# A hybrid decoder step: three GLA projection passes that load x already split in two, with sums moved from GpSimd to VectorE and another product order in the attention pass

## The chip, the core and the metric

The kernel runs on one core of a Trainium2 chip. The metric is the device time of one execution in microseconds (us); the times shown are medians of runs. PE is TensorE's matrix multiply, PEld its weight load, DVE is VectorE, ACT is ScalarE, POOL is GpSimd, and SP is the engine whose queue issues nearly all DMAs here.

## The reference

One decoder layer for 2048 prompt tokens and 64 sample tokens (8 sequences of 8), model width 1024, all in float32:

```python
z = jnp.einsum('btd,dn->btn', x, w_in)
q, k, v, g_att, gq, gk, gv, g_gla, g_lr, r_att, r_gla = jnp.split(z, SPLIT_POINTS, axis=-1)
o_att = swa_prompt(q, k, v, attn_sink, rel_table)      # or swa_sample; 8 heads of 64, window 128
log_a = log_sigmoid(g_lr @ w_gk_up + b_gk) / 16
o_gla, S = gla(gq * HK**-0.5, gk, gv, log_a, s0)       # 4 heads, state 128 x 256
o_gla = o_gla * rsqrt(mean(o_gla**2) + EPS) * gla_norm_w
h_att = (o_att * silu(g_att)) @ w_pa
h_gla = (o_gla * silu(g_gla)) @ w_pg
merged = sigmoid(r_att) * h_att + sigmoid(r_gla) * h_gla
x = layer_norm(DN_ALPHA * x + merged @ w_o, ln_g, ln_b)
```

The GLA recurrence of a head, by chunks, with b the running sum of log_a: `o = (q e^b) S + tril((q e^b)(k e^-b)^T) v`, and S is decayed and gains `(k e^(b_last-b))^T v`. Outputs are the new x, the last keys and values, and the states.

## The kernel before

**Products.** Every float32 product is made of three fast ones. An operand a is split into a high part (`xh`, `wh`: a ScalarE cast, line 144) and a low part (`xl`, `wl`: the difference, line 145, on VectorE or GpSimd), and high x high, low x high and high x low are summed in PSUM (lines 1126 to 1128).

**Passes.** The projections go in eight passes: AT (attention columns of `w_in`, five column groups p), G0, G1, G2 (the GLA columns, four groups each), then `w_pa` (half the depth), `w_ra`, `w_rg`, `w_pg`. A pass does a two-by-two block product in seven products instead of eight. Product i uses one combination of x's blocks and one of the weights'; products 1, 2 and 3 use plain blocks of x, the others combinations kept in DRAM (`xc_d`), made once while AT starts. Tokens come in MS = 3 stripes s, so a pass has 7 x 3 units (i, s), and a unit has one group of 12 matmuls per p, 128 x 128 by 128 x 352 (6 in `w_pa`).

**Operands of a unit.** `raw_x` loads 704 KB into a buffer `xs`, `prep_x` splits it into `xh` and `xl`. All three come from one set of seven buffers, `xb`. x's low part is made on VectorE in AT and after G2, on GpSimd in G0, G1 and G2 (`eng=nc.gpsimd`). All seven combinations are the same in AT, G0, G1, G2, w_ra and w_rg. Loads of x are issued up to three units ahead, splits one unit ahead. Weights: `raw_w` loads one to three blocks, `prep_w` combines them on GpSimd (lines 176 to 182) and splits them, a product ahead.

**Combination of the products.** `combine` takes each group out of PSUM. With the order 1, 2, 7, 6, 5, 3, 4, product 1 is copied to `a12`; 2 completes a quadrant; 7 is copied by ScalarE to `a21` (line 239); 6 is added to `a12` (line 242), and GpSimd adds that sum to `a21` (line 243); 5 completes a quadrant (246) and is added to `a12` (247); 3 (250) and 4 (253) complete the last two. A finished quadrant goes to its sink: a store, or a tanh and a VectorE product (`silu_sink`, line 270) and a store.

**Other work on TensorE.** Its order is written out: after each full group of products `tick` issues what stands due at that tick. The attention runs from two ticks before the end of AT to somewhere in G1. The recurrence follows (`chain`), from then to 12 ticks before `w_pg`: one head after another, tile after tile of 128 tokens, in steps of `st` ticks. For a tile, `gla_a` makes the masked matrix A, `gla_v` transposes v and k and has ScalarE copy them (line 891, tiles `ak` and `gv`), `gla_b` multiplies (lines 921 to 924) and starts the norm (`gla_norm`: ScalarE square, line 908, two GpSimd steps on one column, lines 909 and 910, ScalarE scaling into `ring`, line 911), and `gla_c` transposes the normed rows (line 937). `combo` makes the combinations of later passes' operands. Only TensorE's order is fixed by hand; that of the other engines and of SP's queue is laid out when the program is built, from estimated times.

The end, from about 1731 us, is the product with `w_o` and the layer norm.

Of the kernel before, what the change touches and what calls it, by code (L numbers as in the profile page):

```python
# [12 lines left out]
F32 = mybir.dt.float32  # L13
# [8 lines left out]
P = 128  # L22
# [25 lines left out]
GCH = [(i * GT, GT) for i in range(NP // GT - 1)] + [(NP - 2 * P, P), (NP - P, P + NS)]  # L48
GU = GT
NW4 = 10  # L50
ORDER = (1, 2, 7, 6, 5, 3, 4)
FINAL = {2: (0, 0), 5: (1, 1), 3: (0, 1), 4: (1, 0)}


# [1 line left out]
def kernel(ctx, tc, io):  # L56
# [69 lines left out]
    def at(t, fn):  # L126
        side.setdefault(max(int(t), now[0]), []).append(fn)
# [15 lines left out]
    def split(dst_h, dst_l, src, eng=nc.vector):  # L143
        pin["a"] = nc.scalar.copy(dst_h, src)  # L144
        i = eng.tensor_tensor(dst_l, src, dst_h.bitcast(F32), ALU.subtract)  # L145
        if eng is nc.vector:
            pin["d"] = i
# [3 lines left out]

    class Pass:

        def __init__(self, w, kh, np_, src, kept, sinks, parts=None, eng=nc.vector):
            self.w, self.kh, self.np, self.src, self.kept = w, kh, np_, src, kept
            self.sinks, self.parts, self.eng = sinks, parts, eng
            self.A, self.acc = {}, {}

        def wtile(self, tag, p, dt=F32):
# [11 lines left out]
            return out  # L171

        def prep_w(self, i, p, r):
            A, tt = self.A, nc.gpsimd.tensor_tensor
            if i == 7:
                tt(r[0], r[0], r[1], ALU.subtract)  # L176
            elif i == 6:
                tt(r[0], r[0], r[1], ALU.add)  # L178
                tt(r[2], r[0], r[2], ALU.subtract)
                A[p, "s1"], A[p, "s2"] = r[0], r[2]  # L180
            elif i == 3:
                tt(r[0], r[0], A.pop((p, "s2")), ALU.subtract)  # L182
            a = A[p, "s2"] if i == 6 else A.pop((p, "s1")) if i == 5 else r[0]
            hi, lo = (self.wtile(n, p, F32R) for n in ("wh", "wl"))
            split(hi, lo, a)
            return hi, lo

        def raw_x(self, i, s):
            n = self.kh * T
            x = mtile("xb", F32, "xs")[:, :n]  # L190
            if i in (1, 2, 3):
                k, t = {1: (0, 0), 2: (1, 0), 3: (1, 1)}[i]
                if self.src is None:
                    for h in (2 * k, 2 * k + 1):
                        need(ug_d[h], [0], toks(s, t).start, toks(s, t).stop)
                    d = [ug_d[h][:, :, toks(s, t)] for h in (2 * k, 2 * k + 1)]
                else:
                    d = [self.src[:, k * self.kh:(k + 1) * self.kh, toks(s, t)]]
            else:
                assert (id(self.kept), s) in made  # L200
                d = [self.kept[{6: 0, 5: 1, 4: 2, 7: 3}[i]][:, s, :self.kh]]
            m = self.kh // len(d)
            for j, d_ in enumerate(d):
                pin["x"] = nc.sync.dma_start(x.rearrange("p (k t) -> p k t", t=T)[:, j * m:(j + 1) * m], d_)
            return x

        def prep_x(self, i, s, x):
            hl = [mtile("xb", F32R, n)[:, :self.kh * T] for n in ("xh", "xl")]
            split(*hl, x, self.eng)
            return hl  # L210

        def partners(self, i, p, s):
# [9 lines left out]
            nc.sync.dma_start(y.rearrange("p (a t) -> p a t", a=2), d)  # L222
            return [y[:, :T], y[:, T:]]

        def atile(self, p, tag):
            return mtile(tag) if p < 4 else mt("a5", T, 6)

        def combine(self, i, p, s, ps, parts):
            acc, z = self.acc, None
            add = nc.vector.tensor_tensor  # L230
            if i == 1:
                a = acc[p, s, 12] = self.atile(p, "a12")
                nc.scalar.copy(a, ps)
            elif i == 2:
                z = mtile("fin")
                add(z, acc[p, s, 12], ps, ALU.add)
            elif i == 7:
                u = acc[p, s, 21] = self.atile(p, "a21")
                nc.scalar.copy(u, ps)
            elif i == 6:  # L240
                a, u = acc[p, s, 12], acc[p, s, 21]
                add(a, a, ps, ALU.add)  # L242
                pin["p"] = nc.gpsimd.tensor_tensor(u, u, a, ALU.add)  # L243
            elif i == 5:
                a, z = acc[p, s, 12], mtile("fin")
                add(z, acc[p, s, 21], ps, ALU.add)
                add(a, a, ps, ALU.add)
            elif i == 3:
                z = acc.pop((p, s, 12))
                add(z, z, ps, ALU.add)  # L250
            else:
                z = acc.pop((p, s, 21))
                add(z, z, ps, ALU.subtract)
            if z is not None:
                c, t = FINAL[i]
                self.sinks[p](z, parts, p, c, toks(s, t))

    def keep_sink(dst):
# [36 lines left out]
    for h in range(GH):  # L295
        gsinks += [keep_sink(z_kq[h]), keep_sink(z_vv[h]), silu_sink(z_gg[h], nw_h)]
    xT = io["xT"]
    passes = [Pass(io["w_at"], 4, 5, xT, xc_d, [keep_sink(z_kv)] + [keep_sink(z) for z in z_q] +
                   [silu_sink(z) for z in z_ga])]
    passes += [Pass(io[f"w_g{j}"], 4, 4, xT, xc_d, gsinks[4 * j:4 * j + 4], eng=nc.gpsimd) for j in range(3)]  # L300
    passes += [Pass(io["w_pa"], 2, 4, ua_d, ac_d, [store_sink] * 4),
               Pass(io["w_ra"], 4, 4, xT, xc_d, [gated_sink] * 4, parts=ha_d),
               Pass(io["w_rg"], 4, 4, xT, xc_d, [gate_sink] * 4),
               Pass(io["w_pg"], 4, 4, None, uc_d, [merge_sink] * 4, parts=tt_d)]
    P_AT, P_G0, P_G1, P_G2, P_PA, P_RA, P_RG, P_PG = range(8)
    units = [(passes[0], i, s) for s in range(MS) for i in ORDER[:2]]
# [83 lines left out]
    def combo(key, eng):  # L390
        combine_do(*combine_load(combos[key].popleft()), eng)
# [601 lines left out]
    def chain(h, t0, st):  # L993

        at(t0 - 14, lambda: gla_w(h))
        for c, (c0, T_) in enumerate(GCH):
            last = c == len(GCH) - 1
            Tp = T_ - (NS if last else 0)
            nt = Tp // P
            B = dict(h=h, t0=c0, T=T_, Tp=Tp, nt=nt, last=last)  # L1000
            b = t0 + st * (c0 // P)
            at(b - 14, lambda B=B: gla_load(B))
            at(b - 10, lambda B=B: gla_z(B))
            at(b - 10, lambda B=B: gla_load_v(B))
            at(b - 4, lambda B=B: gla_kq(B))
            for i in range(nt):
                o = b + st * i
                at(o, lambda B=B, i=i: gla_a(B, i))
                at(o + st / 4, lambda B=B, i=i: gla_v(B, i))
                at(o + 3 * st / 4, lambda B=B, i=i: gla_b(B, i))  # L1010
                at(o + 3 * st / 2, lambda B=B, i=i: gla_c(B, i, P, i * P))
            at(b + 3, lambda B=B: gla_load_g(B))
            o = b + st * nt
            if last:
                at(o - 5, lambda B=B: samp_state(B))
                at(o - st / 2, lambda B=B: gla_v(B, B["nt"]))
                at(o, lambda B=B: samp_a(B))
                at(o + 1, lambda B=B: nc.sync.dma_start(io["o_sp"][B["h"]], R["S"][sstate[B["h"]]]))
                at(o + 3, lambda B=B: samp_b(B, 0))
                at(o + 5, lambda B=B: samp_b(B, 2))  # L1020
                at(o + 9, lambda B=B: gla_c(B, "s", NS, B["Tp"]))
                at(o + 9, lambda B=B: gla_store(B))
            else:
                at(b + st * (nt + 1 / 2) + 1, lambda B=B: gla_store(B))

    tg = max(tick_of(P_G1) + 2, t_att + 3)
    at(tg, lambda: mpool("cg"))
    at(tg, rings)
# [337 lines left out]
```

## Time and profile before

| | |
|---|---|
| median of 3 runs | 1926.25 us (1920.5 to 1927.8) |
| profiled execution | 1930.8 us, its span 1929.0 us |
| TensorE busy | 1803.9 us, 94% of the span |
| VectorE, ScalarE, GpSimd busy | 69%, 48%, 36% |
| mean granted TensorE clock | 0.978 |
| DMA | 422.65 MB, mean 219 GB/s |

Times are busy times of one profiled execution. A busy TensorE is not TensorE at its peak, since matmuls overlap. In a group's row stand the line, engine, operation, output and inputs, shapes, count, busy us, the mean ns of one, and after the second bar the idle time of the engine before it, with what ended most of it. In a row of a stretch stand its length, each engine's busy us with the count, the granted clock (1.00 is full), the share of time in which the 16 DMA engines worked, and GB/s. A row of waits has who waited, for whom, total us, how many times, and the longest. A helper's line number serves all its callers, so groups are told by their tiles.

### The profile page before, as it was taken

The page shows a single profiled execution, that of the slowest core. Times are in us where ns is not written, and L with a number is a line of the kernel's source. Part 1 is how long each engine was busy: PE and PEld are TensorE (multiplying, and loading weights), DVE is VectorE, ACT ScalarE, POOL GpSimd, SP SyncE. Part 2 cuts the span into 40 slices and gives each one's busy share as a digit, 9 for nine tenths or more (in the row PEclk, how much of TensorE's full clock was granted, in tenths as well). Part 3 has the DMA queues.
Part 4 walks back from the last instruction along what each step waited for, and adds up shares of the span by engine and source line. Part 5 has one row for each costly group of instructions (what it writes and reads, how often), then busy time and mean ns, then how long its engine had stood idle before and what let it go on. Part 6 is the DMA issues. An engine that isn't in the chain of part 4 may idle for free.

```text
span 1929.0 us, 30434 instructions
## 1 busy us (share of the span) xinstructions
PE 1803.9 (94%) x10619; PEld 1638.7 (85%) x10619; DVE 1334.9 (69%) x2372; ACT 921.6 (48%) x1882; POOL 693.3 (36%) x572
## 2 busy tenths in 40 slices
PE   7899989999999998989999999998989999999998
PEld 6699988888878987888888989997889999997886
DVE  5756637787676875658767876887668666876656
ACT  3332235555655455666665656665647433211100
POOL 1253144434344445554424053224342125541111
PEclk9999999999999999999999999999999999999999
DMA  8866766366566676536666987687876888796531
GB/s 301 288 214 207 242 209 200 124 201 209 158 208 205 220 251 208 188 118 183 209 206 180 289 298 229 209 286 267 276 254 204 268 277 281 237 307 222 164 115 55
DMA packets 279641, 422.65 MB, mean 219 GB/s; under 512 B 26509, under 2 KB 221445, under 8 KB 279472
## 3 DMA queue, kind: packets, MB, share of 16 engines
q1 hardware_dynamic: 278560, 419.86, 67.1%
q8 instruction: 84, 1.38, 0.3%
q0 software_dynamic: 832, 0.72, 0.2%
q14 instruction: 69, 0.57, 0.1%
q10 hardware_dynamic: 96, 0.13, 0.0%
HBM read 299.13 MB, written 122.36 MB: 219 GB/s over the span
## 4 chain that ended last, share of the span: by engine, by line
PE 56%; DVE 11%; DMA 10%; ACT 7%; POOL 5%; issue 4%; SPq 1%; DVEq 0%; POOLq 0%; ACTq 0%
PE pd L1126 12%; PE pd L1127 12%; PE pd L1128 11%; PE pd L1173 3%; PE pd L1172 3%; PE pd L1171 3%; DMA ws<-w_g 2%; POOL xl L145 1%; PE pa L587 1%; DVE wl L145 1%; PE pa L621 1%; PE pa L637 1%; DMA x<-ug_d 1%; PE pa L923 1%; DVE xl L145 1%
## 5 line engine op out<-in xcount | busy, mean ns | idle before, releaser
L1126 PE MATMUL pd<-xh,wh 128*128 128x352 f32 x2484 | 854.6, 344 | 35.6 <-ACT xh L144 13.1
L1127 PE MATMUL pd<-xl,wh 128*128 128x352 f32 x2484 | 811.3, 327 | 15.9 <-POOL xl L145 11.6
L1128 PE MATMUL pd<-xh,wl 128*128 128x352 f32 x2484 | 809.9, 326 | 0.1
L1126 PEld LDWEIGHTS pd<-xh,wh 128*128 128x128 f32 x2484 | 476.4, 192 | 85.9 <-issue 32.5
L1127 PEld LDWEIGHTS pd<-xl,wh 128*128 128x128 f32 x2484 | 479.1, 193 | 21.7 <-POOL xl L145 13.2
L1128 PEld LDWEIGHTS pd<-xh,wl 128*128 128x128 f32 x2484 | 475.4, 191 | 0.4 <-DVE wl L145 0.4
L145 POOL TENSOR_TENSOR xl<-xs,xh 128x1408 fp32r<-128x1408 f32 x63 | 206.7, 3281 | 190.5 <-ACT xh L144 164.7
L144 ACT CAST xh<-xs 128x1408 fp32r<-128x1408 f32 (+1 forms) x162 | 208.8, 1290 | 115.7 <-PE pd L1127 101.7
L145 DVE TENSOR_TENSOR wl<-ws,wh 128x512 fp32r<-128x512 f32 (+1 forms) x231 | 200.0, 876 | 62.8 <-ACT wh L144 62.7
L145 DVE TENSOR_TENSOR xl<-xs,xh 128x1408 fp32r<-128x1408 f32 (+1 forms) x99 | 157.8, 1594 | 51.5 <-ACT xh L144 50.6
L144 ACT CAST wh<-ws 128x512 fp32r<-128x512 f32 (+1 forms) x231 | 133.9, 592 | 107.5 <-PE pd L1127 73.5
L243 POOL TENSOR_TENSOR a<-a,a 128x352 f32<-128x352 f32 x99 | 108.5, 1106 | 117.4 <-DVE a L242 104.2
L911 ACT ACTIVATE ring<-pa,sq 128x256 f32<-128x256 f32 (+1 forms) x68 | 32.3, 474 | 168.7 <-POOL sq L910 168.7
L1171 PE MATMUL pd<-woh,x 128*128 128x512 f32 x256 | 101.2, 395 | 0.9 <-ACT woh L144 0.9
L1172 PE MATMUL pd<-woh,x 128*128 128x512 f32 x256 | 101.5, 396 | 0.5 <-DVE x L145 0.5
L1173 PE MATMUL pd<-wol,x 128*128 128x512 f32 x256 | 101.2, 395 | 0.6 <-DVE wol L145 0.6
L178 POOL TENSOR_TENSOR ws<-ws 128x512 f32<-128x512 f32 (+1 forms) x32 | 43.9, 1373 | 152.0 <-DMA ws<-w_pg 36.7
L909 POOL TENSOR_SCALAR sq<-sq 128x1 f32<-128x1 f32 (+1 forms) x68 | 28.6, 421 | 185.2 <-ACT ring L908 185.2
L176 POOL TENSOR_TENSOR ws<-ws 128x512 f32<-128x512 f32 (+1 forms) x32 | 42.3, 1323 | 140.0 <-DVE xl L145 39.5
L601 ACT ACTIVATE s<-s,nm 128x256 f32<-128x256 f32 (+1 forms) x128 | 62.5, 490 | 57.0 <-DVE nm L598 57.0
L144 ACT CAST x<-xst 128x384 fp32r<-128x384 f32 (+2 forms) x48 | 22.3, 486 | 139.3 <-PE pd L1172 104.5
L182 POOL TENSOR_TENSOR ws<-ws 128x512 f32<-128x512 f32 (+1 forms) x32 | 49.6, 1559 | 86.3 <-DMA ws<-w_pa 17.5
(250 smaller groups left out, 2858.1 us busy)
## 6 DMA issues: line engine op xcount, KB each, us to landing
xs<-xc_d SPq DMA_DIRECT2D x72, 704.0 KB
xs<-xT SPq DMA_DIRECT2D x48, 704.0 KB
ws<-w_g SPq DMA_DIRECT2D x108, 256.0 KB
xc<-tt_d SPq DMA_DIRECT2D x48, 352.0 KB
ws<-w_at SPq DMA_DIRECT2D x45, 256.0 KB
ws<-w_ra SPq DMA_DIRECT2D x36, 256.0 KB
ws<-w_rg SPq DMA_DIRECT2D x36, 256.0 KB
ws<-w_pg SPq DMA_DIRECT2D x36, 256.0 KB
```

Of the source, the lines that this page charges most:

```text
L144: pin["a"] = nc.scalar.copy(dst_h, src)
L145: i = eng.tensor_tensor(dst_l, src, dst_h.bitcast(F32), ALU.subtract)
L178: tt(r[0], r[0], r[1], ALU.add)
L182: tt(r[0], r[0], A.pop((p, "s2")), ALU.subtract)
L243: pin["p"] = nc.gpsimd.tensor_tensor(u, u, a, ALU.add)
L601: nc.scalar.activation(sl, sl, AF.Exp, bias=nm[:, h:h + 1], accum_out=sm[:, h:h + 1])
L1126: mm(ps, wh[:, ks], xh[:, ts], start=(k == 0), stop=False)
L1127: mm(ps, wh[:, ks], xl[:, ts], start=False, stop=False)
L1128: mm(ps, wl[:, ks], xh[:, ts], start=False, stop=(k == q.kh - 1))
L1171: mm(ps, xh[:, xs], hi, start=(k == 0), stop=False)
L1172: mm(ps, xl[:, xs], hi, start=False, stop=False)
L1173: mm(ps, xh[:, xs], lo, start=False, stop=(k == KT - 1))
```

## The change

- *Stored operands.* When G0 splits x for products 1, 2, 4, 6 and 7, it also stores both parts to DRAM; AT does so for products 5 and 3. Units of G0, G1 and G2 for which stored parts exist load the two parts, 704 KB each, and split nothing.
- *Engines.* The splits of x that are left are all on VectorE. GpSimd's weight sums are cut in two halves each.
- *Orders.* All passes but AT and `w_pa` go 1, 2, 6, 7, 5, 3, 4: 6 is added to `a12`, and then VectorE writes `a21` as that sum plus 7, so there is no copy of 7 and no GpSimd sum. AT goes 1, 2, 4, 6, 7, 5, 3: ScalarE writes `a21` as minus 4, 6 is added to `a12`, and at 7 VectorE does three additions and completes the quadrant that 4 completed before. `w_pa` keeps the old order and GpSimd's sum.
- *Recurrence.* It starts three ticks later and ends where it did. `gla_v` goes ahead of `gla_a`; `gla_c` comes 15/8 of a step after the tile's start, not 3/2, and the store of a chunk accordingly later.

```diff
-ORDER = (1, 2, 7, 6, 5, 3, 4)
+ORDER = (1, 2, 6, 7, 5, 3, 4)
+OLD = (1, 2, 7, 6, 5, 3, 4)
+FIRST = (1, 2, 4, 6, 7, 5, 3)
...
         def prep_w(self, i, p, r):
-            A, tt = self.A, nc.gpsimd.tensor_tensor
+            A = self.A
+
+            def tt(o, x, y, op):
+                m = self.kh * P // 2
+                for c in (slice(0, m), slice(m, 2 * m)):
+                    nc.gpsimd.tensor_tensor(o[:, c], x[:, c], y[:, c], op)
...
         def raw_x(self, i, s):
             n = self.kh * T
+            if self in split_users and (i, s, "h") in sp_d:
+                hl = [mtile("xb", F32R, n_) for n_ in ("xh", "xl")]
+                for t, n_ in zip(hl, "hl"):
+                    pin["x"] = nc.sync.dma_start(t.bitcast(F32), sp_d[i, s, n_])
+                return hl
...
         def prep_x(self, i, s, x):
+            if type(x) is list:
+                return x
             hl = [mtile("xb", F32R, n)[:, :self.kh * T] for n in ("xh", "xl")]
-            split(*hl, x, self.eng)
+            split(*hl, x)
+            if self.stores(i):
+                for n, t in zip("hl", hl):
+                    d = sp_d[i, s, n] = dram.tile([P, 4 * T], F32, name=f"sp{i}{s}{n}")
+                    nc.sync.dma_start(d, t.bitcast(F32))
             return hl
...
+        def stores(self, i):
+            return i in ((5, 3) if self is passes[P_AT] else (1, 2, 4, 6, 7) if self is passes[P_G0] else ())
...
+            elif i == 6:
+                a, u = acc[p, s, 12], acc.get((p, s, 21))
+                add(a, a, ps, ALU.add)
+                if self.order is OLD:
+                    nc.gpsimd.tensor_tensor(u, u, a, ALU.add)
             elif i == 7:
-                u = acc[p, s, 21] = self.atile(p, "a21")
-                nc.scalar.copy(u, ps)
-            elif i == 6:
-                a, u = acc[p, s, 12], acc[p, s, 21]
-                add(a, a, ps, ALU.add)
-                pin["p"] = nc.gpsimd.tensor_tensor(u, u, a, ALU.add)
+                a, u = acc[p, s, 12], acc.pop((p, s, 21), None)
+                if u is not None:
+                    z = mtile("fin")
+                    add(z, u, ps, ALU.add)
+                u = acc[p, s, 21] = u if u is not None else self.atile(p, "a21")
+                if self.order is OLD:
+                    nc.scalar.copy(u, ps)
+                else:
+                    add(u, a, ps, ALU.add)
+                if z is not None:
+                    add(z, z, a, ALU.add)
...
+            elif self.order is FIRST:
+                u = acc[p, s, 21] = self.atile(p, "a21")
+                nc.scalar.mul(u, ps, -1.0)
...
-    passes += [Pass(io[f"w_g{j}"], 4, 4, xT, xc_d, gsinks[4 * j:4 * j + 4], eng=nc.gpsimd) for j in range(3)]
+    passes += [Pass(io[f"w_g{j}"], 4, 4, xT, xc_d, gsinks[4 * j:4 * j + 4]) for j in range(3)]
...
-                at(o, lambda B=B, i=i: gla_a(B, i))
-                at(o + st / 4, lambda B=B, i=i: gla_v(B, i))
+                at(o, lambda B=B, i=i: gla_v(B, i))
+                at(o + st / 4, lambda B=B, i=i: gla_a(B, i))
                 at(o + 3 * st / 4, lambda B=B, i=i: gla_b(B, i))
-                at(o + 3 * st / 2, lambda B=B, i=i: gla_c(B, i, P, i * P))
+                at(o + 15 * st / 8, lambda B=B, i=i: gla_c(B, i, P, i * P))
...
-    HS = (t_end - tg - 14) / GH
+    HS = (t_end - tg - 17) / GH
     ST = (HS - 4) / (NP // P)
     for h in range(GH):
-        chain(h, tg + 14 + h * HS, ST)
+        chain(h, tg + 17 + h * HS, ST)
```

More of the change, by code (lines that the diff above doesn't have):

```diff
@@ L116 @@
     tt_d = dram.tile([P, 8, 2, NT], F32, name="tt_d")
+    sp_d = {}
     xc_d = dram.tile([4, P, MS, KT // 2, MT], F32, name="xc_d")
@@ L152, with __init__ @@
     class Pass:
-        def __init__(self, w, kh, np_, src, kept, sinks, parts=None, eng=nc.vector):
+        def __init__(self, w, kh, np_, src, kept, sinks, parts=None, order=ORDER):
             self.w, self.kh, self.np, self.src, self.kept = w, kh, np_, src, kept
-            self.sinks, self.parts, self.eng = sinks, parts, eng
+            self.sinks, self.parts, self.order = sinks, parts, order
             self.A, self.acc = {}, {}
@@ L236, in combine @@
                 add(z, acc[p, s, 12], ps, ALU.add)
-            elif i == 7:
-                u = acc[p, s, 21] = self.atile(p, "a21")
-                nc.scalar.copy(u, ps)
-            elif i == 6:
-                a, u = acc[p, s, 12], acc[p, s, 21]
-                add(a, a, ps, ALU.add)
-                pin["p"] = nc.gpsimd.tensor_tensor(u, u, a, ALU.add)
+            elif i == 6:
[3 more added lines that the diff above has]
+                    nc.gpsimd.tensor_tensor(u, u, a, ALU.add)
+            elif i == 7:
+                a, u = acc[p, s, 12], acc.pop((p, s, 21), None)
[9 more added lines that the diff above has]
+                    add(z, z, a, ALU.add)
             elif i == 5:
                 a, z = acc[p, s, 12], mtile("fin")
-                add(z, acc[p, s, 21], ps, ALU.add)
+                u = acc.pop((p, s, 21)) if self.order is FIRST else acc[p, s, 21]
+                add(z, u, ps, ALU.add)
                 add(a, a, ps, ALU.add)
@@ L254, in combine @@
             if z is not None:
-                c, t = FINAL[i]
+                c, t = FINAL[4 if i == 7 else i]
                 self.sinks[p](z, parts, p, c, toks(s, t))
@@ L298 @@
     passes = [Pass(io["w_at"], 4, 5, xT, xc_d, [keep_sink(z_kv)] + [keep_sink(z) for z in z_q] +
-                   [silu_sink(z) for z in z_ga])]
-    passes += [Pass(io[f"w_g{j}"], 4, 4, xT, xc_d, gsinks[4 * j:4 * j + 4], eng=nc.gpsimd) for j in range(3)]
-    passes += [Pass(io["w_pa"], 2, 4, ua_d, ac_d, [store_sink] * 4),
+                   [silu_sink(z) for z in z_ga], order=FIRST)]
+    passes += [Pass(io[f"w_g{j}"], 4, 4, xT, xc_d, gsinks[4 * j:4 * j + 4]) for j in range(3)]
+    passes += [Pass(io["w_pa"], 2, 4, ua_d, ac_d, [store_sink] * 4, order=OLD),
                Pass(io["w_ra"], 4, 4, xT, xc_d, [gated_sink] * 4, parts=ha_d),
@@ L305 @@
     P_AT, P_G0, P_G1, P_G2, P_PA, P_RA, P_RG, P_PG = range(8)
-    units = [(passes[0], i, s) for s in range(MS) for i in ORDER[:2]]
-    units += [(passes[0], i, s) for i in ORDER[2:] for s in range(MS)]
-    units += [(q, i, s) for q in passes[1:] for i in ORDER for s in range(MS)]
+    split_users = passes[P_G0:P_PA]
+    units = [(passes[0], i, s) for s in range(MS) for i in FIRST[:2]]
+    units += [(passes[0], i, s) for i in FIRST[2:] for s in range(MS)]
+    units += [(q, i, s) for q in passes[1:] for i in q.order for s in range(MS)]
     UP = len(ORDER) * MS
@@ L1023, in chain @@
             else:
-                at(b + st * (nt + 1 / 2) + 1, lambda B=B: gla_store(B))
+                at(b + st * (nt + 7 / 8) + 1, lambda B=B: gla_store(B))
     tg = max(tick_of(P_G1) + 2, t_att + 3)
@@ L1036 @@
     for j in range(6):
-        at(tg + 14 + 3 * HS + 16 + 5 * j, lambda: combo("u", nc.gpsimd))
+        at(tg + 17 + 3 * HS + 16 + 5 * j, lambda: combo("u", nc.gpsimd))
     for s in range(MS):
         for j in range(2):
-            t = tg + 14 + 3 * HS + ST * (2 * (s + 1) * T / P) + 10 + 2 * j
+            t = tg + 17 + 3 * HS + ST * (2 * (s + 1) * T / P) + 10 + 2 * j
             at(t if s < MS - 1 else t_end + 6 + 2 * j, lambda: combo("u", nc.vector))
```

## The prediction

> **What bounds the kernel now.** I read the page first, then its busy times cut at the borders of the eight passes, then who made TensorE wait, then the chain that ended last, then the groups with shapes kept apart.
>
> ```profile
> span 1929.0 us, 30434 instructions
> PE 1803.9 (94%) x10619; PEld 1638.7 (85%) x10619; DVE 1334.9 (69%) x2372; ACT 921.6 (48%) x1882; POOL 693.3 (36%) x572
> ```
>
> TensorE is the bound. The change takes no matmul away, so all it can win is TensorE's waits. By pass, in the order attention (AT), three GLA passes (G0, G1, G2), then w_ra and w_rg (the half-size w_pa pass between them and w_pg behind are left out):
>
> ```profile
> core 0: us, PE busy (x) PEld busy (x) DVE busy (x) ACT busy (x) POOL busy (x), PEclk, DMA share, GB/s
> 4.00:252.00 248.00, 229.39 (x1375) 212.50 (x1376) 160.00 (x252) 82.95 (x144) 73.05 (x70) 0.97 0.75 249
> 252.00:495.00 243.00, 230.47 (x1419) 202.13 (x1417) 168.13 (x291) 131.04 (x330) 100.11 (x49) 0.97 0.60 188
> 495.00:733.00 238.00, 225.22 (x1453) 200.10 (x1450) 176.27 (x299) 127.36 (x289) 102.24 (x53) 0.98 0.65 209
> 733.00:975.00 242.00, 221.36 (x1310) 204.83 (x1309) 153.97 (x309) 147.70 (x293) 116.70 (x90) 0.98 0.58 184
> ...
> 1093.00:1314.00 221.00, 217.19 (x1333) 200.97 (x1332) 175.38 (x366) 147.31 (x293) 67.43 (x72) 1.00 0.81 263
> 1314.00:1549.00 235.00, 215.91 (x1265) 201.78 (x1264) 161.79 (x287) 129.50 (x252) 85.99 (x91) 0.96 0.75 250
> ```
>
> A pass of the same 1008 products takes 221 us for w_ra, whose TensorE idles 4 us at full clock, and 238 to 243 us in the GLA passes, where it idles 13 to 21 us and the granted clock is 0.97 to 0.98. POOL is busiest in just those. The waits, total us, times, longest:
>
> ```profile
> PE pa L937 <- ACT ring L911: 17.2, 8, 4.7
> PE pa L923 <- ACT ak L891: 14.1, 6, 3.8
> ...
> PE pd L1127 <- POOL xl L145: 11.6, 6, 5.8
> PE pa L923 <- ACT gv L891: 7.2, 3, 3.7
> ...
> PE pd L1126 <- DVE a L247: 4.3, 4, 2.6
> ```
>
> Two families: x's low part from POOL (11.6 us) and the recurrence's two ScalarE results, the copied v/k tile (14.1 + 7.2) and the normed row (17.2), together 38.5 us. The chain at the start of G0 shows how the first arises:
>
> ```profile
> 252.22 0.74 ACT xh L144
> ...
> 253.51 6.61 DMA ws<-w_g
> 260.28 0.58 POOL ws L178
> ...
> 261.62 1.26 POOL ws L179
> 262.88 3.11 POOL xl L145
> ```
>
> POOL runs in order. Its sums of raw weights wait for the weights' DMA (6.61 us), and the split of x, whose own input is ready, stands behind them. The same lateness reaches the recurrence's norm, whose two tiny POOL steps feed the ring.
>
> **The change part by part.** Durations by shape:
>
> ```profile
> L145 POOL TENSOR_TENSOR xl<-xs,xh 128x1408 fp32r<-128x1408 f32 x63 | 206.7, 3281 | 190.5 <-ACT xh L144 164.7 <-PE pa L621 8.4 <-PE pa L899 7.1
> L144 ACT CAST xh<-xs 128x1408 fp32r<-128x1408 f32 x141 | 192.4, 1366 | 106.7 <-PE pd L1127 92.7 <-issue 8.3 <-PE pd L1128 3.2
> L145 DVE TENSOR_TENSOR wl<-ws,wh 128x512 fp32r<-128x512 f32 x203 | 184.6, 919 | 59.2 <-ACT wh L144 59.1
> L145 DVE TENSOR_TENSOR xl<-xs,xh 128x1408 fp32r<-128x1408 f32 x78 | 136.5, 1750 | 45.4 <-ACT xh L144 44.6 <-PE pd L1127 0.5
> L243 POOL TENSOR_TENSOR a<-a,a 128x352 f32<-128x352 f32 x99 | 108.5, 1106 | 117.4 <-DVE a L242 104.2 <-DVE ess L723 3.8 <-DVE nm L598 3.6
> ...
> L253 DVE TENSOR_TENSOR a<-a,pd 128x352 f32<-128x352 f32 x93 | 47.1, 513 | 27.6 <-PE pd L1128 27.3
> ...
> L239 ACT COPY a<-pd 128x352 f32<-128x352 f32 x93 | 40.6, 451 | 18.1 <-PE pd L1128 18.1
> L178 POOL TENSOR_TENSOR ws<-ws 128x512 f32<-128x512 f32 x28 | 41.0, 1464 | 130.8 <-DMA ws<-w_pg 36.7 <-DMA ws<-w_g 35.4 <-DMA ws<-w_at 18.1
> ...
> L270 DVE SCALAR_TENSOR_TENSOR fin<-th,fin 128x352 f32<-128x352 f32 x36 | 30.3, 841 | 13.7 <-ACT fin L269 9.7 <-ACT th L267 3.5
> ...
> L178 POOL TENSOR_TENSOR ws<-ws 128x256 f32<-128x256 f32 x4 | 2.9, 736 | 21.2 <-DMA ws<-w_pa 10.7 <-DVE gb L847 10.5
> ```
>
> *Stored operands.* Of the GLA passes' 63 splits, G0 makes 15 (operands 1, 2, 4, 6, 7), now on VectorE. The other 48 units load finished parts, G0's two remaining operands from what AT stored. POOL loses 63 x 3.281 = 207 us, ScalarE 48 x 1.366 = 66 us; VectorE gains 15 x 1.750 = 26 us, all in G0. The path loses the 11.6 us; since G0's splits keep a chain of 1.366 + 1.750 us behind their load, I take -10 (ends 0 and -11.6). What is late next there is the weights' DMA itself, which then delays only its own product, due three units later.
>
> *Sums moved from POOL.* The sum of L243 goes in all passes but w_pa: 87 x 1.106 = 96 us off POOL. In the six passes in the new order a VectorE add takes the place of ScalarE's copy: 72 x 0.513 = 37 us on, 72 x 0.451 = 32 us off ScalarE. Cutting POOL's weight sums in halves costs nothing: 2 x 736 against 1464 ns. For VectorE G0 is the worst: (168 + 26 + 12 x 0.513) / 243 = 0.82, as w_ra now (175.4 / 221 = 0.79, 4 us idle). I take +3 for the GLA passes (ends 0 and +10).
>
> *AT's order 1, 2, 4, 6, 7, 5, 3.* Product 4 needs one raw weight where 7 needed two and a POOL sum: a lighter start, taken at 0. Product 7 now makes three adds a group and finishes a quadrant: over its three units 45 x 0.513 + 6 x 0.841 (the gated outputs) + 3 x 1.750 + 5 x 0.919 = 38 us on VectorE. TensorE needs for the same 180 matmuls, by the last stretch of AT,
>
> ```profile
> 221.00:252.20 31.20, 31.20 (x196) 31.20 (x195) 21.95 (x30) 10.40 (x15) 9.91 (x6) 1.00 0.75 235
> ```
>
> 180 x 31.2 / 196 = 28.7 us. So VectorE is the bound there by 9 us, less what four PSUM buffers of 12 matmuls (7.6 us) let it lag. The next product, 5, has two adds (25 us with the same rest) and pays some back. Ends 0 and +9; I take +4, since today's waits on L247, where a product has two adds, come to 4.3 us in all.
>
> *DMA.* 42 stores and 48 further loads of 704 KB:
>
> ```profile
> xs<-xc_d SPq DMA_DIRECT2D x72, 704.0 KB
> xs<-xT SPq DMA_DIRECT2D x48, 704.0 KB
> ```
>
> 90 x 0.721 = 65 MB more. G1 rises by 15.1 to 64.8 MB, 272 GB/s in 238 us; G2 to 246. Both lie about where w_ra (263) already runs. The tight place is where stores meet AT's end: operands 5 and 3 (split a unit ahead of use) and G0's 1 and 2, 12 units x 1.44 = 17.3 MB in about 185 to 306 us.
>
> ```profile
> 185.00:306.00 121.00, 112.05 (x686) 109.40 (x684) 67.39 (x107) 45.09 (x84) 40.41 (x21) 0.96 0.67 208
> ...
> 1600.00:1620.00 20.00, 17.18 (x105) 16.89 (x106) 14.69 (x19) 5.33 (x8) 8.19 (x6) 1.00 1.00 340
> 1080.00:1100.00 20.00, 20.00 (x125) 18.98 (x124) 17.39 (x35) 13.45 (x26) 1.68 (x3) 1.00 1.00 329
> ```
>
> 208 x 121 = 25.2 MB become 42.5 MB. At the 329 to 340 GB/s of a full DMA that takes 125 to 129 us instead of 121: +4 to +8. With TensorE able to run dry (0 of 20 us at 1080) or not, and late weights of 6.61 us up to three times, ends 0 and +20; I take +7. [...] The rows with share 1.00 stop at 340 GB/s, and the measurement decides.
>
> *The recurrence's ticks.* A tick is a group of 12 matmuls, 235 / 84 = 2.8 us in w_rg. A chunk step was (74.5 - 4) / 16 = 4.41 ticks and becomes 4.36. From the v/k transposes to their use: 1/2 step (2.2 ticks) becomes 3/4 (3.27), 3.0 us more. From the norm's start to its transpose: 3/4 (3.3) becomes 9/8 (4.9), 4.5 us more. The mask's matmul loses 3.1 us of lead to its use, with one 0.3 us VectorE step in it and no wait on it today. Nine waits up to 3.8 us and eight up to 4.7 would nearly all fit. ScalarE also loses its 66 us of casts ahead of these copies, POOL the splits ahead of the norm. But w_ra and w_rg keep the casts, and a wait that goes lets the next come due sooner: I take two thirds, -26 (ends 0 and -38.5), and +2 for the mask (0 to +4) and other misfits.
>
> *Clock.* After such waits TensorE runs slow:
>
> ```profile
> 858.00:872.00 14.00, 10.38 (x55) 9.78 (x54) 8.76 (x24) 6.94 (x15) 9.16 (x9) 0.88 0.25 77
> 255.00:270.00 15.00, 9.21 (x49) 8.91 (x48) 0.00 (x0) 3.08 (x5) 9.64 (x5) 0.77 0.70 226
> 1338.00:1353.00 15.00, 9.51 (x39) 8.46 (x40) 11.14 (x16) 11.07 (x22) 8.75 (x9) 0.77 0.67 223
> ```
>
> These lose 1.7, 3.5 and 3.5 us. G0, G1, G2 and w_rg lose 0.03 x 243 + 0.02 x 238 + 0.02 x 242 + 0.04 x 235 = 26 us in all. Ends 0 and -26; I take -8, a third, as some follows waits that stay and part of each dip falls in idle time. [...]
>
> Sum: -10 + 3 + 4 + 7 - 26 + 2 - 8 = -28 us. The profiled execution took 1930.8 us and becomes 1903; the median of the runs is 1926.25, 4.5 lower, so 1898. All ends together would be 1850 and 1969.
>
> **The rivals.**
> A, slower: loads of x stop the DMA queue. SP issues in order; with pairs, seven x buffers hold three units and one half, so the second load of unit n+3 waits for the end of unit n, and weights and stores behind it wait too. Against it, it waits for x buffers already:
>
> ```profile
> SPq L204 <- POOL xl L145: 180.7, 45, 9.8
> ```
>
> 4.0 us each, with TensorE losing only 11.6; and a loaded pair is ready two units ahead. It decides from (28 + 9.6) / 48 = 0.8 us of TensorE per loaded unit; at 1.3 us it is 62 us: 1960.
> B, no change: the recurrence's waits only move, since its ScalarE and POOL steps keep their order behind other work; without that term and with 2 of the clock's 8: -28 + 26 + 6 = +4, 1930. For it: w_rg keeps all its casts and has the longest waits (4.7).
> C, larger gain: both families go and the clock with them, while DMA alone costs: -11.6 - 38.5 - 20 + 6 = -64, 1862. For it: w_ra shows 221 us for a like pass.
> D, smaller gain: VectorE becomes the bound where sums and splits moved to it, with the terms at +9 and +10 and a little lag after: 1898 + 13 = 1911. Against: fewer POOL operations beside it may shorten its own.
>
> **How the numbers follow.** Forecast 0.47 (1880 to 1916), B 0.17, A 0.14, D 0.12, C 0.10. What a measurement tells from no change is 0.5%, 9.6 us. Faster: 0.47 + 0.10 + 0.10 of D = 0.67. Same: 0.16 of B + 0.02 of D = 0.18. Slower: A and 0.01 of B = 0.15. The range 1868 to 1936 leaves out A and the far part of C.
>
> **What would show it.** POOL's xl rows and ScalarE's 48 casts are gone, 42 stores and 96 loads of 704 KB in their place; no wait of TensorE on POOL xl; waits on ring, ak and gv under 15 us together; G0 to G2 at 225 to 233 us each; AT as long as before or some us longer, with waits on VectorE's adds in product 7; DMA share about 0.9 around 185 to 306 us. Wrong if TensorE waits on xh or xl loaded by DMA, if SP's waits for x buffers hold up the weights, or if the recurrence's waits keep their 38 us.

## The result and the profile after

The changed kernel takes 1910.17 us (median) against 1928.71 us for the kernel before on the same chip: ratio 0.9898, 95% interval 0.9873 to 0.9924. That is 1.0% less, some 20 us. The forecast was 28 us less.

The profiled execution took 1907.78 us, with a span 23.1 us shorter than before. The first lines of its page:

```profile
span 1905.9 us, 30394 instructions
PE 1797.3 (94%) x10619; PEld 1634.6 (86%) x10619; DVE 1281.0 (67%) x2489; ACT 841.6 (44%) x1762; POOL 416.0 (22%) x554
```

TensorE's idle time fell from 125.1 to 108.6 us and its busy time by 6.6 us, with the same matmuls. GpSimd lost 277 us of work, ScalarE 80, and VectorE 54, though VectorE had been given more to do.

Busy times cut at the first product matmul of each pass (AT, G0, G1, G2, then w_ra and w_rg):

```profile
4.70:245.10 240.40, 228.30 (x1377) 211.88 (x1378) 159.72 (x282) 82.06 (x141) 49.84 (x66) 0.98 0.84 287
245.10:499.80 254.70, 234.11 (x1418) 204.11 (x1416) 173.22 (x318) 119.83 (x312) 36.03 (x44) 0.97 0.82 290
499.80:732.10 232.30, 220.03 (x1443) 198.37 (x1441) 147.09 (x311) 98.79 (x256) 18.06 (x26) 0.97 0.79 267
732.10:955.20 223.10, 216.76 (x1309) 202.52 (x1307) 131.17 (x314) 117.81 (x255) 47.62 (x84) 0.98 0.79 271
...
1073.10:1307.00 233.90, 221.21 (x1335) 204.05 (x1334) 179.43 (x382) 146.06 (x282) 53.92 (x85) 0.99 0.78 249
1307.00:1533.70 226.70, 213.43 (x1269) 197.98 (x1269) 149.04 (x296) 122.28 (x236) 70.42 (x94) 0.98 0.78 259
```

Lengths by the same cut, us:

| | AT | G0 | G1 | G2 | w_pa | w_ra | w_rg | w_pg |
|---|---|---|---|---|---|---|---|---|
| before | 247.6 | 243.1 | 237.4 | 242.1 | 118.4 | 220.7 | 235.5 | 181.7 |
| after | 240.4 | 254.7 | 232.3 | 223.1 | 117.9 | 233.9 | 226.7 | 174.3 |

Six passes win 48 us together, G2 most of all; G0 loses 12 and w_ra 13. Who made TensorE wait (total us, times, longest):

```profile
PE pd L1164 <- ACT xh L147: 12.8, 7, 4.7
PE pd L1165 <- DVE xl L148: 12.7, 10, 3.9
PE pa L962 <- DVE aper L939: 12.0, 11, 2.1
PE pa L882 <- DMA gin<-gl_d: 11.5, 3, 5.3
...
PE pa L975 <- ACT ring L949: 4.6, 2, 2.7
PE pa L961 <- ACT gv L929: 2.6, 1, 2.6
PE pa L961 <- ACT ak L929: 2.4, 3, 1.4
...
PE pa L927 <- DVE ring L967: 1.9, 2, 1.6
...
PE pa L937 <- DVE ring L967: 1.4, 1, 1.4
```

The waits on POOL xl are gone, and those on ring, gv and ak fell from 38.5 to 9.6 us. But most of the wait for x's low part only changed hands. VectorE's row for it, 12.7 us now, stood before at

```profile
PE pd L1127 <- DVE xl L145: 3.7, 3, 1.6
```

and in G0 alone, which still splits 15 units, 8.8 us of waits on POOL xl became 8.4 us on VectorE's xl. Two rows are new: `aper`, the masked matrix that VectorE makes for the recurrence, and `gin`, a small input of the gates that comes by DMA.

### The profile page after: what moved, and what is told of

It reads as the page before. It is cut to its first block, busy times and chain, and to the rows that moved or that the text cites. A ratio compares the mean times of both kernels' runs of the same rounds, so it can differ in the third digit from the quotient of the medians.

```text
span 1905.9 us, 30394 instructions
## 1 busy us (share of the span) xinstructions
PE 1797.3 (94%) x10619; PEld 1634.6 (86%) x10619; DVE 1281.0 (67%) x2489; ACT 841.6 (44%) x1762; POOL 416.0 (22%) x554
## 5 line engine op out<-in xcount | busy, mean ns | idle before, releaser
L1165 PE MATMUL pd<-xl,wh 128*128 128x352 f32 x2484 | 809.6, 326 | 13.0 <-DVE xl L148 12.7
L1164 PEld LDWEIGHTS pd<-xh,wh 128*128 128x128 f32 x2484 | 475.5, 191 | 73.5 <-issue 35.2
L182 POOL TENSOR_TENSOR ws<-ws 128x256 f32<-128x256 f32 (+1 forms) x256 | 205.7, 827 | 681.1 <-DMA ws<-w_g 261.0
L148 DVE TENSOR_TENSOR xl<-xs,xh 128x1408 fp32r<-128x1408 f32 (+1 forms) x114 | 175.5, 1539 | 65.9 <-ACT xh L147 61.5
L148 DVE TENSOR_TENSOR wl<-ws,wh 128x512 fp32r<-128x512 f32 (+1 forms) x231 | 158.6, 693 | 80.5 <-ACT wh L147 75.2
L147 ACT CAST xh<-xs 128x1408 fp32r<-128x1408 f32 (+1 forms) x114 | 143.3, 1258 | 85.5 <-PE pd L1165 74.3
L947 POOL TENSOR_SCALAR sq<-sq 128x1 f32<-128x1 f32 (+1 forms) x68 | 23.7, 349 | 461.4 <-ACT ring L946 461.3
L639 ACT ACTIVATE s<-s,nm 128x256 f32<-128x256 f32 (+1 forms) x128 | 62.4, 489 | 40.1 <-DVE nm L636 40.1
L284 DVE TENSOR_TENSOR a<-a,pd 128x352 f32<-128x352 f32 x93 | 47.7, 519 | 34.2 <-PE pd L1166 34.1
L259 DVE TENSOR_TENSOR fin<-a,pd 128x352 f32<-128x352 f32 x99 | 50.7, 516 | 27.6 <-PE pd L1166 23.7
L280 DVE TENSOR_TENSOR fin<-a,pd 128x352 f32<-128x352 f32 x93 | 48.2, 518 | 27.2 <-PE pd L1166 19.8
L256 ACT COPY a<-pd 128x352 f32<-128x352 f32 x99 | 43.4, 450 | 51.4 <-PE pd L1166 51.4
```

Of the source, the lines that this page charges most:

```text
L182: nc.gpsimd.tensor_tensor(o[:, c], x[:, c], y[:, c], op)
L280: add(z, u, ps, ALU.add)
L639: nc.scalar.activation(sl, sl, AF.Exp, bias=nm[:, h:h + 1], accum_out=sm[:, h:h + 1])
L1164: mm(ps, wh[:, ks], xh[:, ts], start=(k == 0), stop=False)
L1165: mm(ps, wh[:, ks], xl[:, ts], start=False, stop=False)
```

## The experiments

Ratios are to the kernel before, with 95% intervals. S stands for the stored operands, O for the new product orders and their VectorE sums, H for GpSimd's weight sums in halves, T for the recurrence's ticks. "Two ahead" is new: pairs of stored parts are loaded at most two units ahead, not three.

| kernel | parts | ratio | interval |
|---|---|---|---|
| after | S O H T | 0.9898 | 0.9873 to 0.9924 |
| a1 | S O H | 0.9858 | 0.9839 to 0.9876 |
| a2 | T | 0.9958 | 0.9938 to 0.9978 |
| a3 | O H T | 0.9957 | 0.9940 to 0.9973 |
| a4 | S | 0.9825 | 0.9805 to 0.9845 |
| b1 | stores only, never read | 0.9976 | 0.9951 to 1.0000 |
| c1 | O | 0.9949 | 0.9925 to 0.9972 |
| d1 | S, AT's order | 0.9806 | 0.9768 to 0.9844 |
| b2 | S, two ahead | 0.9767 | 0.9727 to 0.9807 |
| b4 | S O H T, mask first | 0.9924 | 0.9898 to 0.9950 |
| f3 | S O H T, two ahead | 0.9828 | 0.9802 to 0.9854 |
| f4 | S, AT's order, two ahead | 0.9761 | 0.9737 to 0.9785 |
| f2 | S T, two ahead, mask first | 0.9737 | 0.9711 to 0.9763 |

**The change without its ticks (a1).** The changed kernel with the recurrence timed as before:

```diff
-                at(o, lambda B=B, i=i: gla_v(B, i))
-                at(o + st / 4, lambda B=B, i=i: gla_a(B, i))
+                at(o, lambda B=B, i=i: gla_a(B, i))
+                at(o + st / 4, lambda B=B, i=i: gla_v(B, i))
...
-                at(o + 15 * st / 8, lambda B=B, i=i: gla_c(B, i, P, i * P))
+                at(o + 3 * st / 2, lambda B=B, i=i: gla_c(B, i, P, i * P))
...
-    HS = (t_end - tg - 17) / GH
+    HS = (t_end - tg - 14) / GH
```

> The changed kernel with the recurrence's ticks as before (mask first, v/k transposes a quarter step after, norm's transpose at 3/2 step, start at 14 ticks). Theory 1 (the longer leads ended TensorE's waits on ak, gv and ring): those waits, 9.6 us together in the changed kernel, come back to 25 us or more, the waits on the mask tile (aper, 12.0 us) go, and the time rises by 5 to 20 us over the changed kernel. Rival 2 (freed ScalarE and GpSimd ended them, whatever the ticks): the waits on ak, gv and ring stay under 15 us, aper's 12 us go, and the time is the changed kernel's or up to 8 us less.

Measured 0.9858: faster than the whole change, though the two intervals just touch. On top of the rest the ticks bring nothing and may cost some 8 us. By the time this is rival 2; the waits lie between the bounds of both theories:

```profile
PE pa L975 <- ACT ring L949: 8.7, 5, 6.3
PE pa L961 <- ACT gv L929: 8.5, 3, 4.2
...
PE pa L961 <- ACT ak L929: 3.0, 2, 2.8
```

With the old ticks, the rest of the change has already brought the 38.5 us of these three rows to 20.2. Waits for ScalarE's ring at other matmuls come to 8.8 us more (1.8 before), so all of TensorE's waits on these ScalarE tiles went from 40.3 to 29.0 us. The ticks then take 19 us of these away (9.6 are left), and bring 12.0 us of waits for the mask and 4.3 us more for `gin` (7.2 here, 11.5 in the changed kernel).

**The ticks alone (a2).** The kernel before with the lines above reversed.

> The kernel before with the recurrence's new ticks alone. Theory 1: waits on ak, gv and ring fall from 38.5 us to under 15, and the time falls by 10 to 20 us. Rival 2: they stay over 25 us, and the time falls by less than 6 us or rises by the new waits on the mask.

Measured 0.9958, 8 us less where 26 were forecast. The waits of TensorE:

```profile
PE pa L924 <- DVE aper L901: 15.0, 12, 2.8
...
PE pa L923 <- ACT ak L891: 12.3, 4, 8.2
...
PE pa L937 <- ACT ring L911: 6.9, 4, 4.0
...
PE pa L923 <- ACT gv L891: 2.5, 1, 2.5
```

Ring, ak and gv fall from 38.5 to 21.7 us, between the bounds of both theories, and 15.0 us come back as waits for the mask: the 1/4 step by which `gla_a` was put off is missing between its matmul and `gla_b`.

**The change without the stores (a3).** Nothing is stored, GpSimd splits x in the GLA passes:

```diff
-            split(*hl, x)
+            split(*hl, x, nc.gpsimd if self in split_users else nc.vector)
...
-            return i in ((5, 3) if self is passes[P_AT] else (1, 2, 4, 6, 7) if self is passes[P_G0] else ())
+            return False
```

> The changed kernel without stored operands: every unit of the GLA passes loads x once and splits it on GpSimd as before; orders, sums, halves and ticks as changed. Theory 1 (stored operands gain 11.6 us of GpSimd waits and lose about as much to DMA and to VectorE in G0): G0 is 8 to 15 us shorter than the changed kernel's 255, G1 and G2 longer by 5 to 12 us each, waits on xl from GpSimd back at about 10 us, and the time within 8 us of the changed kernel. Rival 1 (they are the gain): 12 us or more slower than the changed kernel.

Measured 0.9957. Orders, halves and ticks together bring 8 us, no more than the ticks or the orders alone. By the same cut G0 takes 237.3 us, G1 241.4 and G2 240.3: against the changed kernel, G0 is 17 us shorter and G1 and G2 are 9 and 17 longer. The waits on POOL xl were to return to 10 us and are 2.3, although GpSimd splits x again.

**The stored operands alone (a4).** The kernel before with the added lines of `raw_x`, `prep_x` and `stores`, and the splits that are left on VectorE:

```diff
-            split(*hl, x, self.eng)
+            split(*hl, x)
+            if self.stores(i):
+                for n, t in zip("hl", hl):
+                    d = sp_d[i, s, n] = dram.tile([P, 4 * T], F32, name=f"sp{i}{s}{n}")
+                    nc.sync.dma_start(d, t.bitcast(F32))
```

> The kernel before with stored operands alone (all splits that are left on VectorE, old orders, old ticks, whole weight sums). Theory 1: a gain of 0 to 10 us, with G0 no faster than before's 243 us and G1 and G2 faster by 5 us or more each. Rival 1: a gain of 12 us or more. If DMA at its limit outweighs the gain: slower than before by up to 10 us.

Measured 0.9825, 34 us less: more than the whole change. G1 (237.4 to 225.7) and G2 (242.1 to 220.8), cut as above, carry it:

```profile
498.10:723.80 225.70, 218.74 (x1450) 197.46 (x1448) 143.67 (x300) 103.06 (x268) 29.38 (x29) 0.98 0.80 274
723.80:944.60 220.80, 216.75 (x1313) 202.40 (x1310) 135.44 (x307) 124.62 (x271) 57.29 (x75) 0.99 0.82 279
```

And the recurrence's waits, with no tick moved:

```profile
PE pa L953 <- ACT ring L927: 9.8, 5, 3.8
...
PE pa L939 <- ACT ak L907: 4.8, 5, 2.3
PE pa L939 <- ACT gv L907: 4.0, 2, 3.8
```

18.6 us against 38.5: about what the ticks alone did, and without the waits for the mask. A likely reason is that casts and splits no longer stand ahead of the copies and the norm's small steps, or run beside them; no run shows this apart.

**The stores alone, never read (b1).** As a4, but the stored parts aren't entered in `sp_d`, so every unit loads and splits as before, and 42 stores are pure extra traffic.

> The kernel before, which besides stores the 42 pairs' parts to DRAM where the changed kernel does, and never reads them: the price of the stores by themselves (30 MB, in AT's last units and G0). If the full DMA of that stretch costs what the prediction took (+4 to +8 us): 4 to 12 us slower than before, with G0 longer by as much. If DMA has room: within 3 us of before.

Measured 0.9976, no loss. The end of AT and the first unit of G0, where the stores lie closest:

```profile
190.00:247.50 57.50, 57.50 (x359) 57.50 (x358) 37.62 (x56) 19.28 (x28) 5.21 (x3) 1.00 0.88 302
247.50:270.80 23.30, 23.30 (x147) 23.28 (x147) 9.20 (x9) 10.71 (x18) 11.13 (x4) 1.00 1.01 367
```

The DMA engines are full at 367 GB/s and TensorE is busy in all of 23.3 us. The time shows no cost of the stores' traffic. In the profile AT takes 243.0 us (247.6 before) and G0 246.5 (243.1), though no unit does less work: a difference of some 5 us in one pass of one profile says little by itself.

**The orders alone (c1).** The changed kernel with the old ticks, no stores, GpSimd's splits and undivided weight sums.

```diff
-                m = self.kh * P // 2
-                for c in (slice(0, m), slice(m, 2 * m)):
-                    nc.gpsimd.tensor_tensor(o[:, c], x[:, c], y[:, c], op)
+                nc.gpsimd.tensor_tensor(o, x, y, op)
```

> The kernel before with the product orders and VectorE sums alone (whole weight sums, old ticks, no stored operands, GpSimd splits in the GLA passes). The stored operands alone gave 0.9825 of before's time and with orders and halves 0.9858, so as a cost the orders would show here as a ratio of 1.00 or more, with w_ra at 233 us or more (TensorE waiting there on ak, gv and ring again). Rival: alone they gain (AT 5 us shorter, w_pg 5 us), and only collide with the stored operands: a ratio under 0.996.

Measured 0.9949, 10 us less. AT wins 7 us, w_rg 7, w_pg 8; w_ra loses 19 (220.7 to 239.9), in this row:

```profile
1083.60:1323.50 239.90, 225.23 (x1332) 207.97 (x1330) 185.84 (x380) 146.16 (x283) 55.05 (x63) 0.96 0.76 244
```

**The stored operands with AT's order only (d1).** The changed kernel with old ticks and undivided sums, and

```diff
-ORDER = (1, 2, 6, 7, 5, 3, 4)
-OLD = (1, 2, 7, 6, 5, 3, 4)
+ORDER = OLD = (1, 2, 7, 6, 5, 3, 4)
```

> Stored operands with the order 1, 2, 4, 6, 7, 5, 3 in AT alone; all other passes keep the old order with GpSimd's sums, old ticks, whole weight sums. If AT's order gains and the other passes' order costs: AT at 240 us against a4_store_alone's 244, w_ra at 222, and 3 to 6 us under a4_store_alone's 1896. If AT's order is the part that costs: 3 us or more above it.

Measured 0.9806: as the stores alone. AT's order does no harm (AT takes 239.8 us, 244.0 in a4), and w_ra stays at 222.4 us. From here to a1 (0.9858) lie the order of the other passes and the halves; the intervals overlap slightly, but in the profiles w_ra goes from 222.4 to 236.9 us.

**Two ahead (b2, f3, f4).** The changed kernel's new waits led here. SP's queue in the changed kernel:

```profile
SPq L202 <- PE pd L1166: 85.1, 29, 19.8
```

L202 is the load of a stored part: it waits until TensorE has done with the unit whose buffer it takes. One such place in the timeline, first SP's issues, then TensorE's matmuls:

```profile
659.00 0.83 SPq L202 DMA_DIRECT2D xh<-sp32h  x1
663.30 0.32 SPq L202 DMA_DIRECT2D xl<-sp32l  x1
666.72 1.24 SPq L424 DMA_DIRECT2D ac_d<-x  x2
...
669.96 0.43 SPq L861 DMA_DIRECT2D gin<-gl_d  x1
```
```profile
663.11 0.32 PE L1166 MATMUL pd<-xh,wl 128*128 128x352 f32 x1
...
672.58 1.19 PE L882 MATMUL pa<-gin,wgk 32*128 32x256 f32 x2 [5.33 <-DMA gin<-gl_d]
```

The low part for three units later goes out at 663.30, just as the unit that holds its buffer ends. What stands behind it on SP is held up by that, and then by a store of a combination (`ac_d`) that waits for VectorE until 666.72. So `gin` goes out at 669.96, and TensorE stands 5.33 us for it. How much of this place is the pair's the trace doesn't tell; f3 below does for the whole. The edit, in the loop over units:

```diff
+    def pair_ready(n):
+        return n < len(units) and units[n][0] in split_users and units[n][1:] + ("h",) in sp_d
...
-        if n:
+        if n and not pair_ready(n + 3):
```

On the stored operands alone (b2):

> Stored operands alone as in a4_store_alone, but loaded pairs are issued at most two units ahead, not three, so that no load of x waits in SP's queue for the end of a unit. If that queueing (rival A of the prediction) costs what TensorE's 5.1 us of waits on gin show with the clock after them: SP's waits on TensorE's matmuls go, the waits on gin go, and the time is 4 to 12 us under a4_store_alone's 1896. If the third unit's lead was needed: TensorE waits on loaded xh or xl, and the time is equal or more.

0.9767 against 0.9825 without it, some 11 us less, with intervals that just touch. G1 has TensorE busy nearly throughout, and SP's waits fall (a4 had 61.2 us, longest 12.1):

```profile
486.00:701.10 215.10, 214.77 (x1449) 194.16 (x1448) 141.34 (x298) 101.91 (x266) 30.43 (x30) 1.00 0.80 280
```
```profile
SPq L194 <- PE pd L1147: 43.7, 26, 6.9
```

G0 goes from 249.5 to 238.7 us and G1 from 225.7 to 215.1, while G2 goes from 220.8 to 233.0, with 9.4 us of waits on ak, ring and gv in it. Over the kernel these three rows stand at 27.2 us again (a4 had 18.6), and still it is the faster of the two.

On the whole change (f3):

> The changed kernel with loaded pairs issued at most two units ahead. If SP's queue behind the third pair costs in the changed kernel what it cost with the stored operands alone (8 us; here 11.5 us of TensorE's waits on gin and the clock after them): gin's waits under 2 us, G1 at 220 us or less, 8 to 14 us under the changed kernel. If not: within 4 us of it.

0.9828 against 0.9898, intervals apart: 13.5 us. G0 falls from 254.7 to 245.1 us, G1 from 232.3 to 222.2, and the waits that were to go shrink (those on `gin` less than expected, to 6.8 us and not under 2):

```profile
PE pa L885 <- DMA gin<-gl_d: 6.8, 3, 3.7
```
```profile
SPq L202 <- PE pd L1169: 34.6, 28, 7.0
```

On the stored operands with AT's order (f4):

> Stored operands, two units ahead, and AT in the order 1, 2, 4, 6, 7, 5, 3; all else as before. If AT's 3 to 4 us add to it: 1883 to 1886. If the heavy attention steps of G0 meet the same waits earlier and give it back: within 3 us of b2_two_ahead's 1888.

0.9761, the same as b2. AT's order adds nothing beside it.

**The mask first (b4, f2).** If only the mask's lead was wrong, `gla_a` at the tile's start should take away the 12.0 us on `aper`. In the changed kernel (b4):

```diff
-                at(o + st / 4, lambda B=B, i=i: gla_a(B, i))
+                at(o, lambda B=B, i=i: gla_a(B, i))
```

> The changed kernel with the mask's matmul issued together with the v/k transposes at the tile's start, not a quarter step later; all other ticks as changed. If the lead taken from the mask is what made the ticks cost (TensorE waits 12.0 us on aper in the changed kernel): those waits fall under 4 us, and the time comes down by 5 to 10 us, to a1_no_ticks' 1901. If the ticks cost in another way (PSUM buffers held longer, loads behind later stores): aper's waits go or move, and the time stays within 4 us of the changed kernel's 1910.

The gain didn't come: 0.9924 against 0.9898, with intervals that overlap, as the other branch had it. The waits for the mask went, and others took their place:

```profile
PE pa L937 <- ACT ring L949: 7.6, 5, 3.3
PE pa L937 <- DVE ring L967: 7.5, 3, 5.6
PE pa L927 <- DVE ring L967: 6.8, 3, 4.1
```

L927 and L937 are matmuls of `gla_v` and `gla_a` themselves: now these stand and wait in their turn. In the changed kernel they had 1.9 and 1.4 us of such waits for VectorE's ring. On b2, with the new ticks and the mask at the tile's start (f2):

> Stored operands alone, two units ahead (b2_two_ahead, 1888 us), with the new ticks but the mask's matmul at the tile's start. If the longer leads help where the mask keeps its own: the 27 us of waits on ring, ak and gv fall under 12 us and the time to 1875 to 1883. If freed engines already gave what the leads could: within 4 us of 1888.

0.9737, the fastest of all, faster than both kernels; against b2 (0.9767) the intervals overlap, so the share of the ticks in it isn't settled. In its profile TensorE is busy 1785.5 of 1876.0 us.

## Why the prediction was right, and where by luck

The direction was right, and the size near, but by errors that cancel. Rival D's time, 1911 us, lies nearest to the measured 1910, by luck too: of VectorE as the bound the rows show the 8.4 us on its xl in G0, while in AT's product 7, where it was to bind most, TensorE idled 0.8 us. Term by term, with the measured value from the run that has this part alone (ratio less 1, by 1929 us):

| step | forecast | measured |
|---|---|---|
| stored operands, with DMA and VectorE's share | -10 + 7 + 3 = 0 | -34 (a4) |
| recurrence's ticks and the mask | -26 + 2 = -24 | -8 alone (a2), 0 to +8 on the rest (a1 to after) |
| orders | +4 | -10 alone (c1); with the halves on top of S some +10 (d1 to a1, intervals overlap slightly) |
| clock | -8 | in the above; TensorE's busy time -6.6, granted clock 0.978 to 0.979 |
| sum | -28 | -20 |

**Stored operands.** The step that failed most priced them by the wait charged to them, 11.6 us on POOL xl. That row was no price. a3 and c1 bring it to 2.3 and 3.7 us with GpSimd still splitting x, and gain only 8 and 10 us; in the changed kernel it ends, but VectorE's xl row is 9.0 us longer. What the stored operands free reaches further. Without touching the recurrence they lower its waits of 38.5 us, to 18.6 in a4 and to 27.2 in b2, so these are only a part of the gain; and they shorten VectorE's own instructions. Groups of the changed kernel, shapes apart:

```profile
L148 DVE TENSOR_TENSOR wl<-ws,wh 128x512 fp32r<-128x512 f32 x203 | 145.9, 725 | 78.8 <-ACT wh L147 73.8 <-issue 4.3
...
L307 DVE SCALAR_TENSOR_TENSOR fin<-th,fin 128x352 f32<-128x352 f32 x42 | 22.5, 535 | 13.7 <-ACT th L304 7.8 <-ACT fin L306 5.8
```

725 ns where the row before had 919, and 535 where it had 841, for the same shape. In a3, which keeps GpSimd's splits, they take 901 and 718 ns; in a4, which lacks them, 807 and 560. So VectorE in G0 was busy 173 of 255 us (0.68), not 200 of 243 (0.82): rival D's argument against itself was the right one. The 8.4 us on VectorE's xl in G0 are no plain price either: b2, whose 15 splits stand on VectorE as well, has no such wait there. How the 34 us divide between ScalarE's casts, GpSimd's order and VectorE's shorter instructions stays open: a kernel that only moves the splits from GpSimd to VectorE, with nothing stored, was not run.

**Halves.** Cutting GpSimd's weight sums in two was taken to cost nothing, with 736 ns for a half, the fastest of the four rows of that shape (736 to 947). In the changed kernel:

```profile
L182 POOL TENSOR_TENSOR ws<-ws 128x256 f32<-128x256 f32 x224 | 189.3, 869 | 628.6 <-DMA ws<-w_g 261.0 <-ACT a L256 92.8 <-DMA ws<-w_pg 61.4
```

Two halves take 1738 ns, where a whole sum took 1390 to 1653: 23 us more of GpSimd in all. What this costs TensorE no run shows.

**DMA.** The ceiling of 329 to 340 GB/s, read off two rows of share 1.00, was no ceiling. In the changed kernel, the stretch that was to overflow and its densest part:

```profile
185.00:306.00 121.00, 115.26 (x716) 111.30 (x716) 79.39 (x140) 45.90 (x94) 14.24 (x18) 0.99 0.91 332
245.10:268.40 23.30, 23.30 (x148) 23.28 (x147) 6.86 (x7) 10.12 (x17) 3.18 (x5) 1.00 1.00 360
```

The share of 0.9 came as forecast (0.91), TensorE's idle time in the stretch fell from 9 to 6 us, and 360 GB/s pass without a wait. Rows of full share thus range from 329 to 367 GB/s in these runs, so the rate in one of them is no ceiling for another stretch with other transfers.

**AT's order.** AT was to be as long as before or some us longer, with VectorE the bound in product 7; it became 7 us shorter (c1 has that too; with the stored operands it is 4 us in d1 against a4, and nothing in f4 against b2). Product 7 and then 5 in the changed kernel:

```profile
157.10:187.30 30.20, 29.44 (x183) 28.86 (x182) 26.09 (x48) 8.79 (x12) 10.10 (x10) 1.00 0.84 270
187.30:216.30 29.00, 29.00 (x182) 28.74 (x182) 26.11 (x50) 9.19 (x13) 0.00 (x0) 1.00 0.95 334
```

VectorE is busy 26.1 us in each, 52 in both, where 38 and 25 were forecast, and TensorE idles 0.8 us in the first. Up to eight of product 7's 45 additions run in the second stretch, and VectorE's other work was cheaper than priced: some 690 ns for a weight split, not 919, and 524 for a gated output, not 841. What was taken at 0, the lighter start with product 4 in place of 7, goes with most of the gain. The stretch just ahead of it, the second half of AT's products 1 and 2 (their units alternate), in which the next product's weights are made ready, before and after:

```profile
52.70:93.40 40.70, 33.12 (x217) 29.30 (x213) 30.19 (x52) 11.74 (x24) 12.28 (x15) 0.98 0.86 291
```
```profile
52.10:87.70 35.60, 32.89 (x217) 29.33 (x213) 24.78 (x51) 10.84 (x23) 8.54 (x12) 1.00 0.94 320
```

5 us less, with TensorE idle 2.7 us where it idled 7.6. Each kernel with AT's new order shows it (d1 34.7 us, c1 35.2), none without (a4 39.9).

**Ticks.** The waits on ring, ak and gv went below 15 us, as foreseen. But in a4 the stored operands do half of this alone, so a gain was booked for waits that two parts of the change remove. And the mask, put at +2 because "no wait on it today" was read as slack, costs 12.0 us of waits here and 15.0 alone. Waits that only move, as in rival B, are what b4 shows.

**Rival A** was there at a third of its deciding price. SP does stand at the third pair, up to 19.8 us, and `gin` comes late. By f3 this costs 13.5 us, 0.28 us for each of 48 loaded units; 0.8 was needed to decide. "TensorE waits on xh or xl loaded by DMA", named as the sign of a failure, is in no row: it was the small loads behind them that were late. Whether SP's waits held up the weights too, another such sign, no run settles.

**The passes.** G0 to G2 were to be at 225 to 233 us. G1 (232.3) is, G2 (223.1) is just faster, and G0 (254.7) is not. With pairs loaded two ahead (f3) 10 of these 12 us go. The slowest in it is the third product, now 6:

```profile
299.90:352.70 52.80, 41.97 (x226) 35.10 (x225) 36.04 (x64) 24.52 (x60) 10.57 (x13) 0.87 0.81 290
```

```profile
POOL ws L182 <- DMA ws<-w_g: 45.0, 5, 17.3
```

The third product of G0 took 40.1 us before; here GpSimd stands in it for raw weights, up to 17.3 us at once, and the clock falls to 0.87. With two ahead and the old orders it still takes 48.3 us (b2), but there G0's first product has become shorter by as much, 23.4 us for 30.8. Taken together, G0's first three products tell more. They take 100 to 102 us in each kernel with the old order in G0, with stored operands or without (before, a2, a4, b1, b2, d1, f2, f4), 97 to 99 with the new order and nothing stored (a3, c1), and 105 to 108 with both (after, a1, b4, f3). So it is the two together that cost here, some 6 us; which step does it was not found.

**What stays open.** Apart, S, O and T would make 52 us; together they make 20. T overlaps with S in part (a1, a4). But O and T also cost w_ra some 12 us: it takes 220 to 225 us in each kernel with neither (before, a4, b1, d1, b2, f4) and 230 to 240 in each with either. TensorE's listed waits in w_ra are 12.6 us in the changed kernel, 5.0 in a4, spread over eight steps of the recurrence; which comes first was not found. The halves of GpSimd's weight sums were not run alone.

## What to carry to other kernels

Price relief of an engine by all that stands behind it and runs beside it, not by the waits charged to it: here 11.6 us of waits stood for a gain of 34, and most of them came back under another engine's name. When the size or number of loads changes, fit the distance of the prefetch to the buffers: here loads that waited for a buffer, up to 19.8 us, held up what was queued behind them, the small load of `gin` among it, and issuing them a unit later brought 13.5 us (f3). When a step is moved in a written-out order, ask of both its ends what lead they lose, and don't add up two cures of the same wait.

## What the hardware showed beyond that

With the stored operands alone, which take GpSimd's splits of x away (a4), a VectorE product of two SBUF operands, 128x352, fell from 841 to 560 ns, and a difference of two, 128x512, from 919 to 807; in the changed kernel, where most of its sums are gone or halved too, to 535 and 725. Why, no run here shows. The other surprise is the 360 to 367 GB/s of one core's DMA over 23 us, loads and stores mixed, with TensorE busy throughout.
